# Column blocks of the input projection issued in written order, and loads requested some steps sooner

## The chip, the core and the metric

The kernel runs on one core of a Trainium2 chip. A core has a matrix engine (TensorE, PE in the profile, with its weight loads as PEld), three engines for elementwise work (VectorE, DVE; ScalarE, ACT; GpSimd, POOL) and a queue engine (SyncE, SP) from which this kernel starts all its transfers between DRAM and on-chip memory. Each engine works through its own list of instructions from the front; semaphores order one engine's work after another's. The metric is the device time of one execution in microseconds (us). The time before is 2621.93 us, the median of three runs.

## The reference

One layer of a decoder trunk on 2048 positions of width 1024, in float32. Cut to what matters:

```python
mod = silu(c) @ w_ada + b_ada                       # shift, scale, gate, twice
h = rms_norm(x, g_mix) * (1 + sc1) + sh1
p = h @ w_in                                        # one projection, 3088 columns
q_a, k_a, v_a, q_m, k_m, v_m, o_m, u_s, v_s, f_a, i_m, f_m = split(p)
y = concat([forgetting_attention(...),              # 8 heads x 64
            sigmoid(o_m) * rms_norm(mlstm(...)),    # 4 heads x 64, chunk by chunk, with a carried state
            gelu(u_s) * mix(layer_norm(gelu(v_s)))])  # spatial gating in chunks of 128 positions
x = x + gt1 * (y @ w_out)
h = rms_norm(x, g_ffn) * (1 + sc2) + sh2
a, g = split(causal_depthwise_conv(h @ w_up, w_conv, b_conv))
x = x + gt2 * ((silu(a) * g) @ w_down)
```

Nothing of this is changed; the change concerns the stage that computes `p` and, beside it, the mLSTM and the spatial gating.

## The kernel before

**Stages.** The kernel has, one after another, the projection (until about 690 us), the attention, the output projection, and the feed-forward part. Matrix products of float32 accuracy are made of three products of rounded halves (`mm3`, L53 to L56: high by high, low by high, high by low).

**The projection.** `steps` (L1065) runs over two halves of the sequence and, in each, over seven blocks of columns of `w_in`: keys of the mLSTM with the gates (block 0), queries and output gates of the mLSTM (1), values of the mLSTM (2), both inputs of the spatial gating (3), keys (4), queries (5) and values (6) of the attention. A block is eight tiles, each 24 products of 128 rows by up to 512 columns into one of three accumulators in PSUM (`acc`). `products` (L597) issues the 24; after the twelfth it calls `tick(True)` where the block is 512 wide, and `tick()` at the end of the tile. What a tile's sums are used for (`consume`: `use_vm`, `use_sgu`, `use_qk`) comes behind that. The weights of the next block are loaded at the ends of the tiles (`Weights.load`, tiles `wr`) and rounded into halves (`Weights.cast`: `wh` on ACT, then `wl` on DVE) in the fifth to eighth tile and after it.

**What a tick does.** It first calls what `after(n, f)` has left for this tick: the later stages of the spatial gating (`mix`, `turn`), of the attention's queries and keys (`normal`, `turn`). The tick in the middle of a tile then takes one step of `rest_of_mod` (L449): one of 64 tiles of `w_ada` (`wa`) is multiplied into a sum on DVE (`modacc`) and the next one is loaded. Then it takes one step of the first generator in `background`: `rows` (the gates of the mLSTM) or `mlstm` (L921), which handles 512 positions in four chunks of 128: queries by keys (`es`, L983) and queries by state (`ec`, L985), then `nps` and `ups` (L1000, L1004) and the update of the state, then the decays of the next chunk (L936, L937, and four exponentials on ACT, L940), each at one tick; and at the end a norm over the heads: on DVE L1031, on ACT L1035, on DVE L1037, a power on POOL (L1039), a product on DVE (`hq`, L1042), transposes on PE (L1049).

**What sets the order.** The program is written as one list, and a scheduling layer makes each engine's list from it. Unless told otherwise it sorts the instructions by priority and by when its own model of the chip expects them to be ready, so an engine's list can differ much from the written one. Memory is shared by tags with a fixed number of buffers, and a tile whose buffer is still in use waits for it. `small_setup` (L496) loads four rows of convolution weights and turns them with two transposes on PE (L506) and two copies on DVE (L507); it is called after block 2 of the second half (L1107).

Of the kernel before, what the change touches and what calls it, by code (L numbers as in the profile page):

```python
# [33 lines left out]
def trunk(  # L34
# [7 lines left out]
    V, A, G, T = nc.vector, nc.scalar, nc.gpsimd, nc.tensor  # L42
# [35 lines left out]
    ident = cst.tile([P, P], F32, name="ident")  # L78
# [10 lines left out]
    colC = cst.tile([P, 176], F32, name="colC")  # L89
# [285 lines left out]
    def misc_ps():  # L375
        return pp.tile([P, 512], F32, name="mp", tag="mp")
# [25 lines left out]
    def load_x(tt):  # L402
        xt = pool.tile([P, D], F32, name="xt", tag="t4k")
        dma(xt, x[tt * P : (tt + 1) * P, :])
        return xt
# [43 lines left out]
    def rest_of_mod():  # L449

        seq = [(col, k) for col in (3072, 3584, 4096, 4608, 2048, 2560, 5120, 5632) for k in range(KT)]
        tiles = {}

        def load(i):
            if i < len(seq):
                col, k = seq[i]
                tiles[i] = pool.tile([P, 512], F32, name="wa", tag="t2k")
                dma(tiles[i], w_ada[k * P : k * P + P, col : col + 512])

        load(0)  # L460
        for i, (col, k) in enumerate(seq):
            st = tiles.pop(i)
            if k == 0:
                acc = pool.tile([P, 512], F32, name="modacc", tag="macc")
                V.tensor_scalar(acc, st, cs[:, 0:1], None, op0=ALU.mult)
            else:
                V.scalar_tensor_tensor(acc, st, cs[:, k : k + 1], acc, op0=ALU.mult, op1=ALU.add)
            load(i + 1)
            if k == 6:
                brow = pool.tile([1, 512], F32, name="brow", tag="t2k")  # L470
                dma(brow, b_ada[:, col : col + 512])
            if k == 7:
                V.tensor_tensor(acc[0:1, :], acc[0:1, :], brow, op=ALU.add)
                after(2, lambda acc=acc, col=col: columns_or_row(acc, col))
            yield

    def columns_or_row(acc, col):
        kind, half = col // 1024, (col % 1024) // 512
        ps = misc_ps()
        if kind in (2, 5):  # L480
            T.matmul(ps, ones, acc, start=True, stop=True)
            gr = pool.tile([1, 512], F32, name="gr", tag="t2k")
            A.copy(gr, ps[0:1, :])
            dma(gt_d[kind // 3 : kind // 3 + 1, half * 512 : half * 512 + 512], gr)
        else:
            for j in range(4):
                T.matmul(ps[:, j : j + 1], acc[:, j * P : (j + 1) * P], ones[:, 0:1], start=True, stop=True)
            sl = slice(half * 4, half * 4 + 4)
            if kind == 3:
                V.tensor_copy(sh2[:, sl], ps[:, 0:4])  # L490
            else:
                V.scalar_tensor_tensor(
                    a2[:, sl], ps[:, 0:4], 1.0, gf[:, half * 4 : half * 4 + 4], op0=ALU.add, op1=ALU.mult
                )

    def small_setup():  # L496
        for i in range(2):
            r = pool.tile([P, P], F32, name="crow", tag="tmpA")
            if i == 0:
                dma(r[0:44], w_conv[0, 0].rearrange("(k p) -> k p", p=P))  # L500
                dma(r[44:88], w_conv[0, 1].rearrange("(k p) -> k p", p=P))
            else:
                dma(r[0:44], w_conv[0, 2].rearrange("(k p) -> k p", p=P))
                dma(r[44:88], b_conv[0].rearrange("(k p) -> k p", p=P))
            ps = misc_ps()
            T.transpose(ps[:, 0:88], r[0:88, :], ident[0:88, 0:88])  # L506
            V.tensor_copy(colC[:, i * 88 : (i + 1) * 88], ps[:, 0:88])  # L507

    def norm_x(xin):
        for xt in xin:  # L510
# [40 lines left out]
    def make_h(tb, xin=None):  # L551
        xs = xin if tb == 0 else norm_x(xin or [load_x(tb * 4 + i) for i in range(4)])
        for k in range(KT):
            ps = (tr_ps, acc_ps)[k % 2]() if tb == 0 else tr_ps()
            for i in range(4):
                T.transpose(ps[:, i * P : (i + 1) * P], xs[i][:, k * P : (k + 1) * P], ident)
            h32 = pool.tile([P, TB], F32, name="h32", tag="t2k")
            hh = pool.tile([P, TB], F32R, name="hh", tag="hT")
            hl = pool.tile([P, TB], F32R, name="hl", tag="hT")
            A.activation(h32, ps, AF.Identity, bias=sh1[:, k : k + 1], scale=a1[:, k : k + 1])  # L560
            V.tensor_copy(hh, h32)
            V.tensor_tensor(hl, h32, hh.bitcast(F32), op=ALU.subtract)  # L562
            hT[tb, k] = (hh, hl)
# [81 lines left out]
    def after(n, f):  # L645

        pending.append((ticks[0] + n, f))
# [273 lines left out]
    def mlstm(qi):  # L921
        t0 = qi * 512
        neb = nebs[qi % 2]
        ecol, acol, dcol = cols[qi]

        yield
        yield
        H = pool.tile([P, 4, 4, 65], F32, name="H", tag="H")

        got = {}  # L930
# [12 lines left out]
        def load(n):  # L943
            t = t0 + n * P
            kn = pool.tile([P, 256], F32, name="kn", tag="kn")
            dma(kn, km_d[t : t + P, :])
            qT = pool.tile([P, 2, P], F32, name="qT", tag="qT")
            dma(qT, qm_d[:, :, t : t + P].rearrange("j p t -> p j t"))
            for hf in range(2):
                hp = slice(hf * 64, hf * 64 + 64)  # L950
                dma(qzs[n % 2][hp, :, hf, :], qm_d[:, hp, t : t + P].rearrange("j p t -> p j t"))
            v1 = pool.tile([P, 4, 65], F32, name="v1", tag="v1")
            dma(v1[:, :, 0:64], vm_d[t : t + P, :].rearrange("p (h d) -> p h d", h=4))
            V.memset(v1[:, :, 64:65], 1.0)
            got["l", n] = kn, qT, v1

        def turned(n):

            kn = got["l", n][0]
            kps = misc_ps()  # L960
            for j in range(2):
                T.transpose(kps[:, j * P : (j + 1) * P], kn[:, j * P : (j + 1) * P], ident)
            kT = pool.tile([P, 2, P], F32, name="kT", tag="kT")
            A.copy(kT.rearrange("p a b -> p (a b)"), kps[:, 0:256])
            got["k", n] = kT

        load(0)
        load(1)
        yield
        turned(0)  # L970
        yield
# [92 lines left out]
    nb = len(blocks)  # L1064
    steps = [(h, i) for h in range(2) for i in range(nb)]  # L1065
    chores.append(rest_of_mod())
    cur = Weights(blocks[0][0], G, ("q2k",) * 3 + ("qhl",) * 3 + ("wr",) * 2)
    for k in range(KT):
        cur.load()
# [3 lines left out]
    for n, (half, i) in enumerate(steps):  # L1073
        if i == 0:
            make_h(half * 2, x0)
            if half == 0:
                head_setup()
            make_h(half * 2 + 1)
        elif n == nb - 1:
            x0 = [load_x(8 + t) for t in range(4)]  # L1080
        if n == len(steps) - 1:
            while background:
                if next(background[0], True):
                    background.pop(0)
            n_accs[0] = 2
            pool.close("proj_r")
            pp.close("proj_r")
            attention_open_right()

            load_k(0)  # L1090
            first_rows = [], []
            first = [scores(0, tb, load_q(0, tb, "qA"), r) for tb, r in zip((1, 0), first_rows)]
            load_v(0, (0, 1))
            background += first
        nxt[0] = Weights(blocks[steps[n + 1][1]][0]) if n + 1 < len(steps) else None
        blocks[i][1](half, cur)
        started.append(n)
        if nxt[0]:
            nxt[0].cast()
        cur = nxt[0]  # L1100
        if i == 0:
            log_gates(half)
            background += [rows(half * 2), rows(half * 2 + 1)]
        if i == 2:
            background.append(mlstm(half * 2 + 1))
        if n == nb + 2:
            small_setup()  # L1107
# [76 lines left out]
    class Block:  # L1184
# [41 lines left out]
        def turn(self, k):  # L1226
            if self.half == 0:
                hT[k] = pool.tile([P, 1024], F32, name="hz", tag="zy")
            ps = pp.tile([P, 512], F32, name="tps", tag="tps")
            for i in range(4):  # L1230
                T.transpose(ps[:, i * P : (i + 1) * P], self.xn[i][:, k * P : (k + 1) * P], ident)
            A.activation(
                hT[k][:, self.half * 512 : self.half * 512 + 512], ps, AF.Identity, bias=sh2[:, k : k + 1], scale=a2[:, k : k + 1]
            )
# [503 lines left out]
```

## Time and profile before

| | us |
|---|---|
| runs | 2617.52, 2621.93, 2623.44 |
| the profiled execution | 2624.15 |
| its span, from the first to the last instruction | 2622.1 |
| TensorE busy in the span | 2537.9 (97%) |
| VectorE, ScalarE, GpSimd busy | 2003.8, 1274.6, 398.3 |
| blocks 1 to 5 of the projection, first half | from about 81 to 338 |
| the same, second half | from about 421 to 674 |

The profile is of one execution. A row of a table by stretches gives the stretch, its length, the busy time and number of instructions (x) of PE, PEld, DVE, ACT and POOL, the granted clock of TensorE as a share of full speed, the mean busy share of the DMA engines and GB/s. A row of the waits says which engine and line waited for what, the sum, how often, and the longest. A row of groups has line, engine, operation, out<-in, shapes and number, then the busy time and the mean in ns of one, then the idle time before them and what ended it. A row of a timeline has start, length, engine and line, and in brackets the idle time before.

### The profile page before, as it was taken

The page shows a single profiled execution, that of the slowest core. Times are in us where ns is not written, and L with a number is a line of the kernel's source. Part 1 is how long each engine was busy: PE and PEld are TensorE (multiplying, and loading weights), DVE is VectorE, ACT ScalarE, POOL GpSimd, SP SyncE. Part 2 cuts the span into 40 slices and gives each one's busy share as a digit, 9 for nine tenths or more (in the row PEclk, how much of TensorE's full clock was granted, in tenths as well). Part 3 has the DMA queues.
Part 4 walks back from the last instruction along what each step waited for, and adds up shares of the span by engine and source line. Part 5 has one row for each costly group of instructions (what it writes and reads, how often), then busy time and mean ns, then how long its engine had stood idle before and what let it go on. Part 6 is the DMA issues. An engine that isn't in the chain of part 4 may idle for free.

```text
span 2622.1 us, 36482 instructions
## 1 busy us (share of the span) xinstructions
PE 2537.9 (97%) x12537; PEld 2102.2 (80%) x12537; DVE 2003.8 (76%) x3438; ACT 1274.6 (49%) x2424; POOL 398.3 (15%) x532
## 2 busy tenths in 40 slices
PE   5999999999999999999989999999999999999999
PEld 5887888878787787777768888888888888888787
DVE  7756647465378888866679888888888888898797
ACT  4433243433278878844555454444444444444443
POOL 2012310022246656620000000000000000000000
PEclk9999999999999999999999999999999999999999
DMA  7544653444564446256723222246222227658523
GB/s 247 160 142 141 180 154 123 143 127 125 165 173 110 127 122 176 55 174 233 268 67 110 83 79 89 81 170 216 88 84 77 89 65 263 227 170 294 184 95 117
DMA packets 302593, 379.58 MB, mean 145 GB/s; under 512 B 31935, under 2 KB 194589, under 8 KB 300361
## 3 DMA queue, kind: packets, MB, share of 16 engines
q1 hardware_dynamic: 302408, 377.26, 45.5%
q8 instruction: 99, 1.62, 0.3%
q14 instruction: 86, 0.70, 0.1%
HBM read 276.44 MB, written 100.74 MB: 144 GB/s over the span
## 4 chain that ended last, share of the span: by engine, by line
PE 77%; DVE 10%; DMA 6%; issue 3%; ACT 2%; POOL 2%; SPq 0%; DVEq 0%; ACTq 0%; POOLq 0%
PE ub L56 11%; PE ub L55 10%; PE ub L54 10%; PE acc L54 5%; PE acc L56 5%; PE acc L55 5%; PE db L55 4%; PE db L56 4%; PE db L54 4%; PE sp L206 3%; PE tp L259 3%; PE op L245 2%; PE op L246 2%; PE wps L56 2%; PE wps L55 2%
## 5 line engine op out<-in xcount | busy, mean ns | idle before, releaser
L54 PE MATMUL acc<-wh,hh 128*128 128x512 f32 (+2 forms) x768 | 287.5, 376 | 1.9 <-DVE vhl L758 1.2
L54 PE MATMUL ub<-T,wsph 128*128 128x512 f32 x704 | 274.2, 390 | 5.8 <-ACT wsph L1350 5.8
L56 PE MATMUL acc<-wh,hl 128*128 128x512 f32 (+2 forms) x768 | 275.8, 363 | 0.3 <-DVE hl L562 0.3
L55 PE MATMUL acc<-wl,hh 128*128 128x512 f32 (+2 forms) x768 | 275.5, 361 | 0.0
L56 PE MATMUL ub<-T,wspl 128*128 128x512 f32 x704 | 273.7, 389 | 1.6 <-DVE wspl L1351 1.6
L55 PE MATMUL ub<-T,wsph 128*128 128x512 f32 x704 | 273.9, 389 | 0.0
L55 PE MATMUL db<-wspl,wsph 128*128 128x512 f32 x616 | 240.4, 390 | 2.8 <-DVE wspl L1482 2.7
L56 PE MATMUL db<-wsph,wspl 128*128 128x512 f32 x616 | 239.6, 389 | 0.0
L54 PE MATMUL db<-wsph 128*128 128x512 f32 x616 | 238.3, 389 | 0.3 <-ACT wsph L1481 0.3
L1350 ACT CAST wsph<-S 128x512 fp32r<-128x512 f32 x176 | 109.7, 623 | 228.7 <-PE ub L55 162.8
L263 DVE TENSOR_TENSOR plo<-tp,phi 128x512 fp32r<-128x512 f32 (+1 forms) x320 | 187.0, 607 | 31.8 <-ACT phi L262 29.5
L54 PE MATMUL ub<-B,wsph 128*128 128x512 f32 x528 | 207.1, 392 | 2.8 <-ACT wsph L1350 2.8
L56 PE MATMUL ub<-B,wspl 128*128 128x512 f32 x528 | 207.2, 392 | 0.6 <-DVE wspl L1351 0.6
L55 PE MATMUL ub<-B,wsph 128*128 128x512 f32 x528 | 207.0, 392 | 0.0
L223 ACT ACTIVATE L<-L,nm 128x1024 f32<-128x1024 f32 (+2 forms) x192 | 172.5, 902 | 36.2 <-DVE nm L212 34.3
L259 PE MATMUL tp<-ident,L 128*128 128x128 f32 x1088 | 177.0, 274 | 3.0 <-POOL L L228 1.2
L262 ACT CAST phi<-tp 128x512 fp32r<-128x512 f32 (+1 forms) x320 | 160.0, 521 | 40.1 <-PE tp L259 38.8
L206 PE MATMUL sp<-kk,q 128*128 128x512 f32 (+3 forms) x640 | 169.3, 375 | 3.4 <-DVE nm L212 2.4
L228 POOL TENSOR_SCALAR L<-L,rs 128x1024 f32<-128x1024 f32 (+2 forms) x192 | 167.6, 884 | 11.0
L1481 ACT CAST wsph<-act 128x512 fp32r<-128x512 f32 x132 | 82.2, 623 | 179.0 <-PE db L55 162.3
L56 PEld LDWEIGHTS acc<-wh,hl 128*128 128x128 f32 x768 | 146.5, 192 | 22.7 <-DVE hl L562 0.8
L54 PEld LDWEIGHTS acc<-wh,hh 128*128 128x128 f32 x768 | 147.7, 193 | 20.9 <-DVE vhl L758 1.4
(334 smaller groups left out, 5951.6 us busy)
## 6 DMA issues: line engine op xcount, KB each, us to landing
w<-in_w_up_dram SPq DMA_DIRECT2D x88, 512.0 KB
wd<-in_w_down_dram SPq DMA_DIRECT2D x176, 256.0 KB
wa<-in_w_ada_dram SPq DMA_DIRECT2D x96, 256.0 KB
act_d<-yc SPq DMA_DIRECT2D x44, 512.0 KB
act<-act_d SPq DMA_DIRECT2D x44, 512.0 KB
wr<-in_w_in_dram SPq DMA_DIRECT2D x64, 256.0 KB
q<-q_d SPq DMA_DIRECT2D x128, 128.0 KB
hc_d<-hl SPq DMA_DIRECT2D x28, 512.0 KB
```

The lines of the kernel that those rows point to most:

```text
L54: T.matmul(ps, lh, rh, start=start, stop=False, skip_group_check=resume)
L55: T.matmul(ps, lh, rl, start=False, stop=False, skip_group_check=resume)
L56: T.matmul(ps, ll, rh, start=False, stop=stop, skip_group_check=resume)
L206: T.matmul(sp[:, b : b + bw], q2[n][:, qs], kk[:, s0 + b : s0 + b + bw], start=n == 0, stop=n == 1 and not last)
L223: A.activation(L[c], L[c], AF.Exp, bias=nm[:, n - 1 : n], scale=-1.0, accum_out=rs[:, c : c + 1])
L228: G.tensor_scalar(t, t, rs[:, 0:1], 1.0, op0=ALU.mult, op1=ALU.mult)
L245: T.matmul(op[:, c0:], vv[:, j, :], hi[:, c0:], start=(j == 0), stop=False)
L259: T.transpose(tp[:, i * P : (i + 1) * P], rows[i][j // 8][:, (j % 8) * P : (j % 8 + 1) * P], ident)
L262: A.copy(hi[:, c0:], tp[:, c0:])
L263: V.tensor_tensor(lo[:, c0:], tp[:, c0:], hi[:, c0:].bitcast(F32), op=ALU.subtract)
L1350: A.copy(hi, src)
L1481: A.copy(hi, v)
```

## The change

From the second to the sixth block of each half (block numbers 1 to 5), everything that is issued stands on each engine's and queue's list in the order in which it is written (`tc.manual_schedule()`), and not in the scheduling layer's own. Around that, three things move in the written order: `mlstm` requests its first two chunks at its first step and yields afterwards, where it yielded twice first; `small_setup` still requests its rows at the same place but turns them four and six ticks later; `rest_of_mod` requests its first tile of `w_ada` and then yields, so that all its steps come one later. Instructions are the same in number and kind on every engine.

```diff
@@ rest_of_mod
         load(0)
+        yield
         for i, (col, k) in enumerate(seq):
@@ small_setup
+        def turn(i, r):
+            ps = misc_ps()
+            T.transpose(ps[:, 0:88], r[0:88, :], ident[0:88, 0:88])
+            V.tensor_copy(colC[:, i * 88 : (i + 1) * 88], ps[:, 0:88])
+
         for i in range(2):
...
-            ps = misc_ps()
-            T.transpose(ps[:, 0:88], r[0:88, :], ident[0:88, 0:88])
-            V.tensor_copy(colC[:, i * 88 : (i + 1) * 88], ps[:, 0:88])
+            after(4 + 2 * i, lambda i=i, r=r: turn(i, r))
@@ mlstm
         ecol, acol, dcol = cols[qi]
-
-        yield
-        yield
         H = pool.tile([P, 4, 4, 65], F32, name="H", tag="H")
...
         load(0)
         load(1)
+        yield
+        yield
         yield
         turned(0)
@@ the loop over steps
+    written = ExitStack()
...
         nxt[0] = Weights(blocks[steps[n + 1][1]][0]) if n + 1 < len(steps) else None
+        if i == 1:
+            written.enter_context(tc.manual_schedule())
         blocks[i][1](half, cur)
         started.append(n)
         if nxt[0]:
             nxt[0].cast()
         cur = nxt[0]
+        if n in (nb - 2, 2 * nb - 2):
+            written.close()
```

## The prediction

> **What bounds the kernel now.** I read the page first, then the two stretches that the change touches, then TensorE's waits in them, then the granted clock behind each wait.
>
> ```profile
> span 2622.1 us, 36482 instructions
> ## 1 busy us (share of the span) xinstructions
> PE 2537.9 (97%) x12537; PEld 2102.2 (80%) x12537; DVE 2003.8 (76%) x3438; ACT 1274.6 (49%) x2424; POOL 398.3 (15%) x532
> ```
> ```profile
> 81.00:338.00 257.00, 248.34 (x1323) 210.49 (x1323) 159.71 (x345) 87.41 (x165) 52.56 (x41) 0.97 0.50 149
> 421.00:674.00 253.00, 246.16 (x1304) 206.98 (x1302) 148.11 (x325) 85.52 (x163) 51.23 (x41) 0.98 0.41 122
> ```
>
> TensorE is busy in 97% of the span, and in blocks 1 to 5 of the two halves it idles 8.7 and 6.8 us; DVE is busy for 62% and 59%, ACT and POOL less. So TensorE's own list sets the time of this stage; every microsecond for which it waits is one of the total, and there are not many. But the clock is 0.97 and 0.98 here. The waits of TensorE in the two stretches:
>
> ```profile
> PE mps L985 <- ACT M L940: 4.6, 1, 4.6
> PE trp L731 <- DVE sy L732: 3.4, 1, 3.4
> PE mps L1049 <- DVE hq L1042: 0.6, 1, 0.6
> ```
> ```profile
> PE trp L731 <- DVE sy L732: 4.0, 1, 4.0
> PE mp L506 <- DVE colC L507: 2.7, 1, 2.7
> ```
>
> Four waits make nearly all of the idle time. The stretches directly behind each of the four:
>
> ```profile
> 160.50:166.00 5.50, 5.50 (x15) 4.53 (x16) 3.24 (x8) 2.59 (x5) 1.67 (x2) 0.50 0.48 146
> 235.80:241.00 5.20, 5.10 (x12) 3.57 (x13) 4.07 (x10) 0.37 (x1) 2.07 (x1) 0.50 0.73 244
> 493.10:497.20 4.10, 4.10 (x16) 3.01 (x17) 1.81 (x4) 2.04 (x4) 0.00 (x0) 0.58 0.91 297
> 574.30:579.00 4.70, 4.60 (x11) 3.21 (x12) 3.57 (x8) 0.37 (x1) 2.07 (x1) 0.50 0.66 214
> ```
>
> After each, TensorE is granted half its clock for some microseconds. That costs (1 - clock) times the length: 2.75 + 2.6 + 1.7 + 2.35 = 9.4 us. The waits themselves are 4.6 + 3.4 + 2.7 + 4.0 = 14.7 us. Together 24.1 us hang on four places.
>
> **Why those four waits are there.** The second one: the spatial gating's `mix` on PE needs a PSUM bank that DVE empties at L732, and DVE does this late:
>
> ```profile
> 232.41 0.69 DVE L772 TENSOR_TENSOR qn<-acc,ss 128x512 f32<-128x512 f32 x1 [1.53 <-POOL ss L128]
> 233.02 2.32 DVE L467 SCALAR_TENSOR_TENSOR modacc<-wa,cs,modacc 128x512 f32<-128x512 f32 x3
> 235.25 0.42 DVE L732 TENSOR_TENSOR sy<-trp,gsgu 128x256 f32<-128x256 f32 x1
> ```
>
> Ahead of it the scheduling layer has put a wait for POOL and a run of `modacc` steps, which nothing needs before the feed-forward part. The 4.0 us wait is the same line, half a sequence later. The first one is a transfer's:
>
> ```profile
> 148.26 2.07 SPq L458 DMA_DIRECT2D wa<-in_w_ada_dram  x3
> ```
> ```profile
> 157.31 0.62 ACT L591 CAST wh<-wr 128x512 fp32r<-128x512 f32 x1 [0.39 <-DMA wr<-in_w_in_dram]
> 157.94 1.28 ACT L940 ACT_TABLE_LOAD   x1
> 159.24 1.14 ACT L940 ACTIVATE M<-mps,acol 128x128 f32<-128x128 f32 x4
> ```
>
> SP requested runs of `wa` tiles ahead of the next block's weights, ACT stood at the rounding of a late weight tile, and the exponentials for which PE waited stood behind it. The 2.7 us wait is a copy on DVE (L507) behind the same kind of rounding.
>
> **The change, part by part.** *Written order.* TensorE's list in the built program keeps its order; only the small products at L487, L481 and L506 move. DVE, ACT, POOL and SP are reordered: one `modacc` step per tile, in its place, and one `wa` request per tile. So runs of them cannot stand ahead of `sy` or ahead of the weights: the waits of 3.4 and 4.0 go, and that of 4.6 goes since block 2, being narrow, has no `wa` requests left in it. I take -4.6 - 3.4 - 4.0 and the clock behind them, -2.75 - 2.6 - 2.35; the bounds are all of it and nothing.
>
> *`small_setup` later.* The same two transposes and copies, four and six ticks after the request: -2.7 and -1.7 for the clock. The four small transfers stay where they were. Its cover is two to three tiles of products; without it the 4.4 us come back.
>
> *`mlstm` sooner.* Ten transfers per call are requested two ticks earlier and pass, on SP, the requests for the last weight tiles of block 2. The three `wa` requests above took SP 0.69 us each, so the weights could be 7 us later; but the last ones wait in any case for the buffers that the roundings of the eighth tile free. I take 0; the other end is the whole first wait with its clock again, 7.35 us in each half.
>
> *`rest_of_mod` one step later.* 66 steps instead of 65 in 72 middle ticks up to block 5 of the second half; its results are used in the feed-forward part. 0; if a step were lost behind the end, it would fall to block 6, where steps are also taken.
>
> *What written order brings on.* A list in written order waits at its head. Three places, the same in each half; these rows price them:
>
> ```profile
> L128 POOL TENSOR_TENSOR ss<-ss,nhalf 128x8 f32<-128x8 f32 x29 | 51.1, 1763 | 128.6 <-DVE ss L767 128.6
> L128 POOL TENSOR_TENSOR mu<-mu,nhalf 128x4 f32<-128x4 f32 x16 | 16.9, 1056 | 20.4 <-DVE mu L713 20.4
> L1039 POOL TENSOR_TENSOR mss<-mss,nhalf 128x16 f32<-128x16 f32 x4 | 12.3, 3080 | 5.8 <-DVE mss L1038 5.8
> L708 POOL TENSOR_TENSOR ev<-ev 128x256 f32<-128x256 f32 x16 | 11.1, 694 | 157.7 <-DVE ev L706 88.3 <-DMA qT<-qm_d 59.2 <-DVE den L1028 3.8
> ```
> ```profile
> L592 DVE TENSOR_TENSOR wl<-wr,wh 128x512 fp32r<-128x512 f32 x68 | 44.9, 686 | 17.2 <-ACT wh L591 17.1
> L467 DVE SCALAR_TENSOR_TENSOR modacc<-wa,cs,modacc 128x512 f32<-128x512 f32 x49 | 36.7, 750 | 18.7 <-DMA wa<-in_w_ada_dram 18.0
> L772 DVE TENSOR_TENSOR qn<-acc,ss 128x512 f32<-128x512 f32 x29 | 20.1, 692 | 45.4 <-POOL ss L128 45.4
> L766 DVE TENSOR_REDUCE ss<-qsq 128x8 f32<-128x512 f32 x29 | 19.8, 681 | 21.4 <-ACT qsq L764 21.0
> ```
> ```profile
> 217.42 1.23 DVE L1042 TENSOR_TENSOR hq<-H,mss 128x1024 f32<-128x1024 f32 x1 [2.46 <-POOL mss L1039]
> ```
> ```profile
> 219.11 0.47 PE L487 MATMUL mp<-ones,modacc 128*128 128x1 f32 x3
> 219.44 0.52 PE L1049 MATMUL mps<-ident,hq 128*128 128x128 f32 x3
> ```
>
> (a) *End of the first mLSTM call, in block 3.* Now `hq` starts directly when POOL's power ends, is done at 218.65, and PE comes at 219.44. Written, a variance of the spatial gating and a `modacc` stand ahead of `hq`, and that variance waits for POOL's square, which stands behind the power. That adds 0.69 (the square), about 0.5 (two short DVE instructions on half the elements of the 0.68 reduction), 0.75 and some 0.3 for three handovers, 2.2 us: `hq` ends at about 220.9. PE comes about 0.8 us sooner, as the products at L487 no longer stand there: 218.65. A wait of 2.3 us. Bounds: 0 if the power starts 2.3 us sooner, and 5 if DVE is as much behind.
>
> (b) *First chunk of the second call, in block 4.* ACT now squares the tile (`qsq`) first:
>
> ```profile
> 242.66 0.60 ACT L764 ACTIVATE qsq<-acc 128x512 f32<-128x512 f32 x1 [3.57 <-PE acc L56]
> 243.16 0.68 ACT L784 ACTIVATE qhi<-trp,colA 128x512 fp32r<-128x512 f32 x1
> 243.86 1.28 ACT L940 ACT_TABLE_LOAD   x1
> 245.15 1.14 ACT L940 ACTIVATE M<-mps,acol 128x128 f32<-128x128 f32 x4
> 246.17 0.39 ACT L964 COPY kT<-mp 128x256 f32<-128x256 f32 x1
> ```
> ```profile
> 251.71 0.45 PE L1000 MATMUL mps<-v,sc 128*128 128x65 f32 x3
> ```
>
> Written, `qsq` stands behind the other four, from about 246.5 to 247.1. Then 0.68 + 0.2 on DVE, 1.76 on POOL, 0.69 (`qn`), 0.75 (`modacc`), about 0.7 (the scores, as large as `qn`): 251.9, and 252.4 with handovers, where PE comes at 251.71. I take 0.7; bounds 0 and 2.
>
> (c) *End of the second call, in block 5.* `hq` is late by 0.6 now in the first half. Written, the power for the tile's queries (1.76), `qn` (0.69), `modacc` (about 0.5 for a first step) and a rounding (0.7) stand between POOL's power and `hq`: 3.7 later. DVE's work ahead of the power is free of `modacc` runs: I take 2.3 off, three steps of 0.75. 0.6 + 1.4 = 2.0; bounds 0.6 and 4.3.
>
> Per half 2.3 + 0.7 + 2.0 = 5.0 us, in both 10.0, of which 0.6 is there now: +9.4. A wait of 2.7 us brought 1.7 us of clock, so I count that for one of the two waits (a): +1.7.
>
> **Sum.** -14.7 - 9.4 + 9.4 + 1.7 = -13.0 us. The profiled execution took 2624.15, 2.2 over the median. 2624.15 - 13.0 - 2.2 = 2609.
>
> [...]
>
> **Rivals.**
> *Nearly the whole gain.* DVE reaches (a), (b) and (c) in time, as it does now at (a) and (b). For it: DVE is idle for some 40% of this stage. Against: it idles at heads of its list, 45.4 us for POOL alone. -24.1 - 0.6: 2597.
> *No change.* The first wait and that at L506 are kept by late weights, whatever the order of the requests: DMA is busy for 0.41 to 0.50 and SP issues ten transfers ahead of them. Then 4.6 + 2.75 + 2.7 + 1.7 = 11.75 us stay, and 2609 becomes 2621.
> *Slower.* In blocks 4 and 5 each tile's `qn` waits for ACT, DVE and POOL in turn, and in written order everything on DVE waits behind it. If this round takes longer than PE's tile, PE waits in each tile: 29 tiles by the row of `qn`. At 1.0 us each that is +29, so 2638. It decides from 0.63 us per tile, where the 13 us are used up and 5.2 more. Against it: at (b) the round comes out only 0.7 too long, and that with a table load which the other tiles lack. [...]
>
> **How the numbers follow.** Forecast 0.48 (2602 to 2618 from the bounds of (a) to (c), two thirds of the way), whole gain 0.20, no change 0.14, slower 0.18. 0.2%, about 5.2 us, is what a measurement of this kernel can tell from none. Faster 0.48 + 0.20, same 0.14, slower 0.18. The range of 8 in 10 reaches from just under the whole gain, 2596, to 2630, a third of the slower case beyond the bound: cases of both signs.
>
> **What would show it.** In the changed profile: no wait of PE for `sy` at the spatial gating, none for `M` at the first chunk, none at the convolution rows; clock 1.00 at those places; one `modacc` per tile on DVE; waits of 1 to 3 us of PE for `hq` twice in each half, and under 1 for the scores. The total of PE's idle time in blocks 1 to 5 falls from 15.5 to about 10 us. It is wrong if weights or `wa` tiles land so late that ACT or DVE stand at them, or if PE waits in most tiles of blocks 4 and 5.

## The result and the profile after

The changed kernel takes 2608.89 us in the median of six runs (2606.95 to 2610.55), the kernel before 2617.97 us in six runs beside them (2616.86 to 2623.44): a ratio of 0.996, with a 95% interval of 0.9948 to 0.9973. The forecast was 2609, in a range of 2596 to 2630. The profiled execution of the changed kernel took 2607.8 us. Two lines of its page:

```profile
span 2606.1 us, 36311 instructions
PE 2530.5 (97%) x12521; PEld 2097.9 (81%) x12537; DVE 2010.0 (77%) x3438; ACT 1272.8 (49%) x2424; POOL 402.5 (15%) x532
```

Against the profile before, the span is 16.0 us shorter. TensorE's idle time in the span went from 2622.1 - 2537.9 = 84.2 to 2606.1 - 2530.5 = 75.6, so 8.6 us less of waiting, and its busy time fell by 2537.9 - 2530.5 = 7.4 us. Both come from the stage that was changed. Here are blocks 1 to 5 of the two halves, cut at the first product of block 1 and of block 6, before and then after:

```profile
77.90:335.10 257.20, 248.54 (x1324) 210.71 (x1323) 159.90 (x348) 85.95 (x162) 52.56 (x41) 0.97 0.50 151
417.30:671.10 253.80, 246.96 (x1310) 207.80 (x1309) 149.31 (x326) 86.09 (x165) 50.34 (x41) 0.98 0.41 123
```
```profile
77.90:325.00 247.10, 243.34 (x1316) 207.30 (x1323) 157.53 (x337) 84.10 (x161) 52.43 (x41) 1.00 0.51 151
407.40:654.40 247.00, 243.63 (x1303) 206.07 (x1310) 153.77 (x330) 85.38 (x164) 51.35 (x41) 1.00 0.46 133
```

Together they took 511.0 us before and 494.1 after, 16.9 less: TensorE's idle time fell from 15.5 to 7.1, and its busy time from 495.5 to 487.0. The products are the same (the trace after lacks records of some of them, as the weight loads beside them show), and the clock is 1.00 in both halves, where it was 0.97 and 0.98; so the 8.5 us of busy time are put down to the clock. The rest of the span is 0.9 us longer. TensorE's waits in the first half after, and then in the second:

```profile
PE mps L1052 <- DVE hq L1045: 3.6, 2, 2.7
```
```profile
PE mps L1052 <- DVE hq L1045: 3.2, 2, 2.7
```

All four waits of before are gone (for `M`, twice for `sy`, for the convolution rows). In each half two waits for `hq` stand in their place, 2.7 us at the end of the first mLSTM call and 0.9 or 0.5 at the end of the second. Line numbers are three or four higher than before: L1045 and L1052 are the lines that were L1042 and L1049.

In the new order DVE waits for PE before the first `sy` of block 4, where PE waited for DVE:

```profile
223.65 0.69 DVE L776 TENSOR_TENSOR qn<-acc,ss 128x512 f32<-128x512 f32 x1 [1.57 <-POOL ss L128]
224.25 0.48 DVE L466 TENSOR_SCALAR modacc<-wa,cs 128x512 f32<-128x512 f32 x1
225.19 0.42 DVE L736 TENSOR_TENSOR sy<-trp,gsgu 128x256 f32<-128x256 f32 x1 [0.45 <-PE trp L735]
```

One multiply of the modulation stands directly ahead of `sy`, of which there was a run before. The profiled pair flatters the change: the medians differ by 9.1 us, because the profiled run before was 6.2 above its median and the profiled run after 1.1 below its own. How much of that is clock is not shown: the mean granted clock over the span is 0.993 and 0.997 in these two, and 0.995 in four of the other five runs of the changed kernel.

### The profile page after: what moved, and what is told of

It is laid out like the page before. It is cut to its first block, busy times and chain, and to the rows that moved or that the text cites. A ratio compares the mean times of both kernels' runs of the same rounds, so it can differ in the third digit from the quotient of the medians.

```text
span 2606.1 us, 36311 instructions
## 1 busy us (share of the span) xinstructions
PE 2530.5 (97%) x12521; PEld 2097.9 (81%) x12537; DVE 2010.0 (77%) x3438; ACT 1272.8 (49%) x2424; POOL 402.5 (15%) x532
## 4 chain that ended last, share of the span: by engine, by line
PE 81%; DVE 9%; DMA 4%; ACT 3%; issue 2%; POOL 1%; SPq 0%; DVEq 0%; ACTq 0%; POOLq 0%
PE ub L56 11%; PE ub L54 11%; PE ub L55 11%; PE acc L54 6%; PE acc L56 6%; PE acc L55 6%; PE db L55 4%; PE db L56 4%; PE db L54 4%; PE sp L206 3%; PE tp L259 3%; PE op L245 2%; PE op L246 2%; PE wps L55 2%; PE wps L54 2%
```

## The experiments

The time fits the forecast. The open question is which part of the change makes it: the written order, as the prediction says, or one of the three moves, which it priced at 0, 0 and -4.4. All ratios are to the kernel before, on the same chip. The waits quoted are TensorE's, for the first half (first fence or first lines) and the second; small rows are left out.

### The written order alone, and the moves alone

`e1_order_alone` has the `ExitStack` lines of the diff and none of the three moves; `e2_moves_alone` has the three moves and none of the `ExitStack` lines.

> Written order in blocks 1 to 5 as in the changed kernel, but the three moves undone: mLSTM's first requests two ticks later, the convolution rows turned at once, the w_ada steps one earlier. My theory (the order removes the waits behind runs of w_ada steps, and the moves are what written order needs at block 2): no wait for sy in either half, hq waits as in the changed kernel (2.7 us twice), but TensorE waits 3 to 7 us for the first chunk's data or the late weights after block 2 in both halves and 3 to 6 us for the convolution rows, some with slow clock: 2624 us (2616 to 2634). Rival 1 (the order alone gives the gain, the moves are idle): 2609 us. Rival 2 (the moves alone give it): 2618 us.

> The three moves without the written order. My theory: the waits for sy and for the exponentials stay (11 to 12 us and their slow clock, some 7 us), only the 2.7 us at the convolution rows and 1.7 us of clock go: 2614 us (2611 to 2619). Rival 1 (order alone gives the gain): 2618 us. Rival 2 (the moves give the gain): 2609 us.

The written order alone: 2626.23 us, ratio 1.0019 (1.0007 to 1.0032). The moves alone: 2606.61 us, ratio 0.9949 (0.9934 to 0.9964), as good as the whole change. The waits of the order alone, in the two halves:

```profile
PE mp L487 <- DVE modacc L473: 2.2, 1, 2.2
PE mps L1049 <- DVE hq L1042: 1.7, 1, 1.7
PE acc L54 <- ACT wh L591: 1.5, 1, 1.5
```
```profile
PE mp L506 <- DMA crow<-in_w_conv_dram: 7.2, 1, 7.2
PE mp L481 <- DVE modacc L473: 2.2, 1, 2.2
```

It does take away the waits for `M` and for `sy`. But in written order PE's list stands at the convolution rows until they land, 7.2 us, with a mean clock of 0.68 from 486 to 502 us; in each half it waits 2.2 us for a sum of `modacc`, and in the first 1.5 us for a rounding of late weights at the start of block 3. That refutes a gain of the order by itself, as its theory had it; only the waits for `hq`, 1.7 and 1.1 us, were not the 2.7 of the changed kernel. And in the first half of the moves without it:

```profile
PE trp L735 <- DVE sy L736: 2.6, 1, 2.6
PE mps L988 <- ACT M L941: 0.9, 1, 0.9
```

The wait for `M` fell from 4.6 to 0.9 though the planner still made every list. The waits for `sy` are shorter too, 2.6 and 1.8 us where they were 3.4 and 4.0. So the theory that only the written order removes those waits fell here, and the time lies nearest to the second rival's 2609.

### Two ways of ordering less or later

`e3_tail_later` is the changed kernel with one `yield` more ahead of the transposes of `hq`. `e4_dve_written` has the moves and holds DVE's list alone in written order:

```diff
-            written.enter_context(tc.manual_schedule())
+            written.enter_context(tc.manual_schedule(engines={mybir.EngineType.DVE}))
```

> The changed kernel with one more step between the product hq and its transposes at the end of each mLSTM call. My theory (those four waits of 2.7, 0.9, 2.7 and 0.5 us are only a matter of TensorE coming too soon): all four go, -6.8 us: 2602 us (2600 to 2605). Rival (DVE is behind by more than a step there, or the second call, now a step later, meets other waits): 2607 us or more, with waits of 2 us or more elsewhere in blocks 3 to 6.

> The changed kernel, but written order on VectorE's list alone; the other lists are the scheduling layer's. My theory (the waits for sy come from VectorE's list, the wait for the exponentials from the lists of the queue and ScalarE): no wait for sy, a wait for the exponentials or the late weights after block 2 of 2 to 5 us in at least one half: 2614 us (2610 to 2619). Rival (the order on one engine is not enough, since each list follows the others): waits for sy stay, 2618 us or more. Rival (VectorE's list is the whole of it): 2609 us, no wait after block 2.

The first took 2611.95 us, 0.9971 (0.9959 to 0.9982): no better than the change. The waits for `hq` are gone, but DVE is late for the next thing, the low halves of the weights (`wl`): PE waits for them for 2.9 us in the first half and 2.6 in the second. That is about what the rival had.

The second took 2607.8 us, 0.9951 (0.9937 to 0.9964). It has no wait for `sy`, but waits for `hq` (1.8 us in the first half, 1.4 in the second) and, in the first half, 3.2 us for `wl` in the first tile of block 6, directly behind the written stretch. Its theory, that a wait for the exponentials or for late weights after block 2 would stay, fell: there is none.

So neither a later tail nor a narrower written order is told from the change by its time.

### One move at a time, planned as before

`f1_mlstm_alone`, `f2_setup_alone` and `f3_mod_step_alone` hold one of the three moves each; the last is one line:

```diff
@@ rest_of_mod
         load(0)
+        yield
```

> The three moves together, without the written order, gave 0.9949; this run and the next two hold one move each, planned as before. Here only mLSTM's first two loads are requested two steps sooner. Theory (each move cures its own wait): the wait for M at the first chunk (4.6 us) shrinks to under 1 and the half clock behind it (2.75) goes, the waits for sy (3.4 and 4.0) and at the convolution rows (2.7) stay: about 7 us, 2613 where before is 2620. Rival (the planner makes another order after any edit, and its waits fall where they fall): the waits for sy change as well though nothing near them was moved, and the time is anywhere from 2608 to 2626, with the sum of the three single gains not that of the three together (13.4).

> Only the convolution weights' two small transposes are made four and six steps later. Theory: the wait of 2.7 at the convolution rows and the 1.7 of clock behind it go, the other three waits stay: 2615.6 where before is 2620. Rival (new order after any edit): the wait for M and those for sy differ from 4.6, 3.4 and 4.0 by over 1 us, and the time is not 4.4 below before.

> Only the first multiply of the chain of modacc is taken one step later. Theory: nothing waits for it; all four waits stay: 2620, as before. Rival (new order after any edit): waits for sy or M differ from 3.4, 4.0 and 4.6 by over 1 us, with a time 3 us or more from before.

mLSTM's loads sooner: 2620.17, 1.0002 (0.9992 to 1.0012). The convolution rows later: 2618.6, 0.9999 (0.9989 to 1.0008). The one line: 2611.24, 0.9962 (0.9947 to 0.9977). The product of the three ratios, 0.9963, lies within the interval of the three together, so the gain of the moves is, as far as this resolves, that of the step of `rest_of_mod`; the theory of one cure for each wait missed the time of all three. In f1 and f2 the waits for `M` and for `sy` stay. These are a row of f1 and two of f2 in the first half; in the second, `sy` is at 4.2 us in both:

```profile
PE mps L984 <- ACT M L937: 5.3, 1, 5.3
```
```profile
PE mps L988 <- ACT M L943: 5.0, 1, 5.0
PE trp L734 <- DVE sy L735: 4.0, 2, 3.4
```

The wait at the convolution rows is gone in both, though f1 doesn't touch them; in f2, other waits (1.7 us at the border of the halves, 0.7 for `M`) came instead. So an edit by itself can move a wait, but these two left `M` and `sy` where they were. With the one line, in the two halves:

```profile
PE trp L732 <- DVE sy L733: 2.7, 1, 2.7
PE mps L986 <- ACT M L941: 1.0, 1, 1.0
```
```profile
PE trp L732 <- DVE sy L733: 1.8, 2, 1.1
```

In the profiled executions, one of each kernel, blocks 1 to 5 (cut as above) took 495.2 us with the one line, 495.8 with the three moves and 494.1 with the whole change; 507.2 and 508.3 with the other two moves, and 511.4 with the written order alone, where they took 511.0 before.

Why a step that nothing waits for is worth 8 to 10 us is seen, for the wait for `M`, in SP's queue. These are the requests for `wa` between 138 and 166 us of this kernel, in the view of one tile's instructions (count, lengths in ns, first and last start), and between 138 and 152 us of the kernel before:

```profile
L458 SPq DMA_DIRECT2D wa<-in_w_ada_dram x5: 328/328/611, 138.4 to 165.7; - x5
```
```profile
L458 SPq DMA_DIRECT2D wa<-in_w_ada_dram x10: 328/410/1076, 139.0 to 149.9; - x10
```

Before, ten tiles are requested in that time, ahead of the last weights of block 3; one step later two are, and the other three follow at 162 us and after, behind those weights. The weights land sooner, and ACT's last rounding ahead of the exponentials goes from 157.31 us, in the prediction's rows, to 152.23:

```profile
152.23 0.62 ACT L592 CAST wh<-wr 128x512 fp32r<-128x512 f32 x1 [1.84 <-DMA wr<-in_w_in_dram]
152.87 1.28 ACT L941 ACT_TABLE_LOAD   x1
154.16 1.14 ACT L941 ACTIVATE M<-mps,acol 128x128 f32<-128x128 f32 x4
```

### The dose, and the queue by itself

If the runs of `wa` and `modacc` that get ahead are the cause, a second step should shorten them again, and SP's queue in written order should do without any move. `g3_two_steps` has two `yield`s in place of one and nothing else; `g1_sp_written_only` has no move:

```diff
+            written.enter_context(tc.manual_schedule(engines={mybir.EngineType.SP}))
```

> The one step by which modacc starts later gave 0.9962 alone. Here it starts two steps later, and nothing else is changed. Theory A (the step sets how far the runs of wa requests and modacc multiplies get ahead): the built lists hold, between the fourth and the fifth mixing result of the spatial gating, 7 multiplies in before, 5 with one step, 0 here in the first half, and 5, 1, 0 in the second; PE waited there for 3.4, 2.7 and 4.0, 1.8 us. So here both waits for sy are under 0.5 us with no half clock behind them; the wait for M stays near 1 us. Less than one step: 2.7 + 1.8 + 1.7 = 6.2 us, so 2605 where before is 2620. Theory B (any edit gives another order, and the gain is luck): the waits for sy do not follow the counts, or waits of over 2 us stand at other places; 2608 to 2622.

> No move; only SP's queue of transfers stands in written order in blocks 1 to 5, the other engines stay with the planner. The built queue of before has 11 wa requests between the eighth weight tile of one block and the first of the next, ahead of block 3's weights; here there are 1 and 0. Theory A: the wait for M (4.6) shrinks to 1 or less and its clock (2.75) goes; the runs of multiplies ahead of sy, 7 and 5 in before, are 3 and 3 here, so those waits shrink to about 1.5 us each, without half clock: -7 - 4.4 - 5 = about -15, and 2605 where before is 2620, with the wait at the convolution rows (2.7 and 1.7) as the part that may stay: 2609. Theory C (the transfers are not what ACT waited for): the wait for M stays over 3 us: 2613 or more.

Two steps: 2605.72 us, 0.9947 (0.9929 to 0.9965), where theory A had 2605. SP's queue alone: 2608.12 us, 0.9955 (0.9939 to 0.9971), between the theory's 2605 and 2609. The waits with two steps, in the two halves:

```profile
PE mp L964 <- DVE sh L492: 1.1, 1, 1.1
PE mps L987 <- ACT M L942: 0.8, 1, 0.8
PE trp L733 <- DVE sy L734: 0.4, 1, 0.4
```
```profile
PE mps L938 <- DVE H L1003: 1.0, 1, 1.0
PE trp L733 <- DVE sy L734: 0.4, 1, 0.4
```

No wait is over 1.1 us, where theory B had some of over 2. The run of multiplies that stood ahead of `sy` now comes behind it in the planner's own list, and the clock is 1.00 in both stretches:

```profile
227.98 0.69 DVE L774 TENSOR_TENSOR qn<-acc,ss 128x512 f32<-128x512 f32 x1 [1.53 <-POOL ss L128]
228.59 0.75 DVE L734 TENSOR_TENSOR sy<-trp,gsgu 128x256 f32<-128x256 f32 x2
...
230.11 0.48 DVE L467 TENSOR_SCALAR modacc<-wa,cs 128x512 f32<-128x512 f32 x1
```

So with zero, one and two steps the waits for `sy` in the first half are 3.4, 2.7 and 0.4 us, in the second 4.0, 1.8 and 0.4. The multiplies that DVE ran between the fourth and the fifth `sy` in the traces are those of the expectation: 7, 5 and 0, then 5, 1 and 0. Why the planner places them otherwise after one step is not shown. And with SP's queue alone ordered, PE no longer waits for `M`; 0.9 and 1.9 us in the first tile of block 3, for the rounding of one of the last weight tiles, are what is left of late weights. The two longest rows of each half:

```profile
PE trp L731 <- DVE sy L732: 3.3, 2, 2.5
PE acc L54 <- ACT wh L591: 0.9, 1, 0.9
```
```profile
PE acc L54 <- ACT wh L591: 1.9, 1, 1.9
PE trp L731 <- DVE sy L732: 1.3, 1, 1.3
```

The theory had about 1.5 us for each wait for `sy`: 3.3 and 1.3 were measured, with three multiplies between in either half, so the length of the run alone does not fix them.

### What the move of mLSTM's loads does within the written order

`f4_without_mlstm` is the changed kernel with the two `yield`s of `mlstm` back in their old place.

> The change without its move of mLSTM's loads: written order, convolution weights later, modacc one step later. The written order alone stood at 1.0019 with a wait of 7.2 us at the convolution rows and 5.1 of clock behind it, and 1.5 at the start of block 3. Theory (in written order each move cures its own wait): the wait at the convolution rows goes with its clock, 12 us less than the written order alone: 2613. The 2.2 at the start of block 4 stays. Rival (the move of the loads is what makes the written order bearable, since the transfers ahead of the weights stand in one row): waits of over 1.5 us at the start of blocks 3 and 4 stay and cost clock: 2618 or more.

2615.36 us, 0.9981 (0.9972 to 0.9991): between theory and rival, and slower than the change (0.996) by intervals that just touch. The wait at the convolution rows is gone, as the theory had it; 0.7 and 1.5 us for late weights are left in the first tile of block 3, and no wait for `modacc`, of which it kept 2.2. Here the move seems worth something, though part of the difference may be clock (0.50 behind two of its waits, see the last section). ACT's waits from 470 to 495 us, in this kernel and then in the changed one:

```profile
ACT wh L595 <- DMA wr<-in_w_in_dram: 8.4, 2, 6.0
```
```profile
ACT wh L595 <- DMA wr<-in_w_in_dram: 3.4, 3, 2.7
```

In written order the ten transfers of mLSTM stand between the weight tiles; requested two steps sooner they are through before the last weights are asked for. The planner, with lists of its own, gained nothing by it (f1).

### Two versions made from this

`g4_dve_blocks34` has the moves, and DVE's list in written order in blocks 3 and 4 only. `g6_two_steps_and_moves` has two steps of `rest_of_mod` and the other two moves, and no written order.

> The three moves, with DVE's list alone in written order and in blocks 3 and 4 alone. DVE's written list in all five blocks gave 0.9951 with no wait for sy, but with 0.95 + 2.22 us at the end of block 5 of the first half and 0.99 and 0.60 for hq at the end of the second mLSTM call. Theory A: the waits for sy stay away (no multiply stands between the fourth and fifth mixing result), those of block 5 go, as the planner orders it: 4.8 us less than DVE's list in all blocks, 2602 where before is 2620, and faster than the change. Rival (the border of the written stretch costs what it saves, since what the planner put before it now stands in a run at it): waits of 1 to 3 us at the start of block 3 or 5: 2607 or more.

> modacc two steps later, and the change's two other moves (mLSTM's loads sooner, the convolution weights turned later), all planned, no written order. Theory A (only the place of modacc and wa counts while the planner makes the lists): no waits for sy, M under 1 us, ratio as with two steps alone, 0.9947 +- 0.0015, so 2605 to 2608 where before is 2620. Rival (the two other moves hold a gain of their own once the waits for sy are gone, such as the 0.96 and 1.05 us before the second chunk's products): 0.993 or less, 2602. In either case it is faster than the change if its interval ends below 0.9948.

2604.08 us, 0.9939 (0.9924 to 0.9954), and 2605.22 us, 0.9946 (0.9933 to 0.996). In the first, no wait for `sy` is left and none behind block 5 for the weights, but 3.0 us for `hq` in the first half, which its theory didn't have. The second is as fast as two steps alone: the other moves hold nothing in planned lists. Both, and two steps alone, have a better ratio than the change (0.996), but all the intervals overlap with its own: faster than before is shown, faster than the change isn't.

## Why the prediction was right, and where not

*The four waits, -14.7 us, and the clock behind them, -9.4.* All four are gone, and no half clock is left in the stage (1.00 in both halves). The mechanism, that runs of `wa` requests and `modacc` multiplies stand ahead of weights and of `sy`, held: both doses and SP's queue by itself move the waits. The attribution failed. The step "*`rest_of_mod` one step later* ... 0" was mis-sized: alone it measured a ratio of 0.9962, some 10 us, and the written order, which was to bring the gain, measured 1.0019 alone. The prediction took the written order as the way to break up the runs and asked of the step only who waits for its results. But the generator has 64 multiplies and as many transfers, and where they fall in the planner's lists decides what is late. That nothing needs the multiplies before the feed-forward part was not right either: small products on PE's own list (L481, L487) read `modacc` within these blocks, and with the order alone PE stood at them for 2.2 us in each half; with the step, in the changed kernel and in f4, it does not. Put on top of the moves, the written order adds nothing that the intervals can tell (0.996 against 0.9949).

*`small_setup` later, -4.4.* In planned lists, nothing (0.9999): the wait goes, but any of the three edits removed it, and others came. In the written order without the moves, PE stood there for 7.2 us; in the whole change, and in that without mLSTM's move, not at all. So the move is needed by the written order, and the 4.4 us are no gain of its own.

*`mlstm` sooner, 0.* Right in planned lists (1.0002). In written order it is probably a gain: f4, without it, has 0.9981 against 0.996, 0.2% or some 5 us, with intervals that just touch. The prediction's other end, weights up to 7 us later, had the wrong sign: ACT's wait for them in the second half is 3.4 us with the move and 8.4 without.

*(a), 2.3 us.* Right, 2.69 in each half, and by the chain it was worked out from; the place is the first tile of block 4, not block 3. POOL's square stands behind the power, and `hq` behind the variance that needs the square and behind a multiply:

```profile
207.80 3.27 POOL L1042 TENSOR_TENSOR mss<-mss,nhalf 128x16 f32<-128x16 f32 x1 [3.88 <-DVE mss L1041]
211.04 0.91 POOL L712 TENSOR_TENSOR ev<-ev 128x256 f32<-128x256 f32 x1
```
```profile
211.98 0.42 DVE L716 TENSOR_REDUCE mu<-ev 128x4 f32<-128x256 f32 x1 [0.51 <-POOL ev L712]
212.43 0.17 DVE L717 TENSOR_SCALAR mu<-mu 128x4 f32<-128x4 f32 x1
212.51 0.74 DVE L468 SCALAR_TENSOR_TENSOR modacc<-wa,cs,modacc 128x512 f32<-128x512 f32 x1
213.17 1.22 DVE L1045 TENSOR_TENSOR hq<-H,mss 128x1024 f32<-128x1024 f32 x1
```

*(b), 0.7 us: none. (c), 2.0 us: 0.88 and 0.49.* The scores came in time, and PE waited for the second `hq` about a third as long as worked out; which of the terms taken from block 5 was too large no run tells apart. The handovers, 0.3 us in (a) and 0.5 in (b), are estimates that no run shows; in the rows above, `ev` ends at 211.95 and `mu` starts at 211.98. Together the new waits are 2 x 2.69 + 0.88 + 0.49 = 6.75, of which 0.63 was there: +6.1 for +9.4.

*The clock of (a), +1.7.* None in the profiled run, 1.00 in both halves, while f4 has 0.50 behind the same wait: one row can't price it (last section).

*The sum.* In blocks 1 to 5 the waits give -14.7 + 6.1 = -8.6, and TensorE's idle time fell by 8.4, from 15.5 to 7.1, where the forecast was about 10; the terms (a) to (c) held 3.3 us too much. Its busy time fell by 8.5, where the clock was to give -9.4 + 1.7 = -7.7. So the profiled pair gained 16.9 us in these blocks, and 13.0 were forecast. That the time came out as 2608.89 for 2609 is luck in good part: the drop of 13.0 was taken from a median of three runs, 2621.93, while the six runs beside the changed kernel have 2617.97 and the medians fell by 9.1 (7.1 to 13.6 by the interval). The direction, the end of the four waits and the wait (a) were rightly forecast; the agreement to 0.1 us shows nothing beyond that.

*The rivals.* The whole gain did not come, as (a) and (c) are there. "No change" is refuted by SP's queue alone, which ended the wait for `M`: the order of the requests matters. "Slower" needed a wait in most tiles of blocks 4 and 5, and PE has none for `qn`.

## What to carry to other kernels

Where a scheduling layer makes the lists, look for background work without a due time (here loads and multiplies for a later stage) and count how many of its instructions stand ahead of the late one in each list: moving that work by a step or two gave as much as fixing every list by hand. An order written out by hand removes runs, but a list then stands at its head for a late transfer, as PE did here for 7.2 us at the convolution rows, so other moves had to come with it. Undo each part of such a change alone, since a total that comes out as forecast says little about which part made it.

## What the runs showed of the hardware

The length of a wait alone doesn't tell the clock behind it. The kernel without mLSTM's move waits 2.7 us for `hq` at the same two places as the changed kernel, and behind each wait TensorE is granted half its clock. Here are the stretch in which most of the wait falls and the next, in each half (TensorE's busy time stands behind the first comma, the clock third from the end):

```profile
213.24:216.65 3.41, 0.70 (x6) 0.59 (x6) 3.09 (x6) 1.62 (x4) 1.70 (x2) 1.00 0.92 324
216.65:220.06 3.41, 3.41 (x12) 2.84 (x11) 2.80 (x8) 0.00 (x0) 1.28 (x2) 0.50 0.10 37
547.75:551.16 3.41, 1.44 (x7) 0.85 (x5) 2.87 (x6) 2.28 (x5) 2.67 (x3) 1.00 0.72 194
551.16:554.57 3.41, 2.68 (x11) 2.51 (x12) 3.05 (x7) 0.00 (x0) 1.04 (x2) 0.50 0.56 201
```

Priced as the prediction does it, (1 - clock) times the length, that is 1.7 us in each half over these 3.41 us. In the changed kernel the clock stays at 1.00 through the same wait and behind it, in either half:

```profile
211.00:217.00 6.00, 3.31 (x19) 2.61 (x18) 5.31 (x11) 2.28 (x5) 2.89 (x4) 1.00 0.65 219
543.00:549.00 6.00, 3.31 (x19) 2.76 (x19) 5.06 (x11) 1.60 (x4) 2.64 (x3) 1.00 0.58 212
```

And behind the wait of 2.7 us at the convolution rows before, it was 0.58 over 4.1 us (the prediction's row at 493.10). So of these five waits of 2.7 us, three had a lowered clock behind them and two had not. What decides between them is not shown, nor whether the same wait costs clock in one execution and none in the next, since each kernel has one profiled execution.
